# Seven block products for eight in 39 tiles of a feed-forward product, and TensorE makes the last shift

## The chip, the cores and the metric

One core of a Trainium2 chip runs the whole program. The metric is device microseconds for one execution, as the median of several runs. The program is a two-layer encoder in float32. TensorE (PE) gets each float32 operand as two parts: a high part `h` (the value cast to the matmul format) and a low part `lo` (what the cast lost). A product is the sum of three matmuls: high by high, low by high, high by low.

## The reference, cut to what matters

```python
DEPTH, D_MODEL, D_FF, SEQ, N_META = 2, 2048, 8192, 256, 16
def _layer(h, w_in, ..., ln1_w, ln1_b, w_ff1, w_ff2, ln2_w, ln2_b):
    ...                                             # projections, two mixers, output projection
    h = _layer_norm(DEEPNORM_ALPHA * h + mix, ln1_w, ln1_b)
    ff = jnp.einsum('blf,fd->bld', jnp.square(jax.nn.relu(jnp.einsum('bld,df->blf', h, w_ff1))), w_ff2)
    return _layer_norm(DEEPNORM_ALPHA * h + ff, ln2_w, ln2_b)
```

The case is about the last `einsum` of layer two, by `w_ff2`: 256 tokens by 8192 by 2048 columns. In layer two the 16 meta tokens are no longer carried, so there are 256 rows.

## The kernel before

**Stages.** Layer two's feed-forward runs in two halves of 4096 hidden columns. A half makes its hidden activations (`ev_f` squares the rectified result and splits it into the pairs `u[k]`, 32 chunks of 128 columns; in the listings they are called `y0` to `y15` and `u16` to `u31`), and then calls `across(u, half, g)` four times, once for each group `g` of 512 output columns. "The second product" below means these eight calls.

**A tile.** `across` runs over 16 weight tiles. A tile holds two chunks of 128 rows by 512 columns, 1024 floats in each of 128 partitions. For a tile, TensorE makes 12 matmuls of 512 columns: two token halves of 128, two chunks, three parts. Here the activations are the stationary operand (they are loaded as weights) and the weight tile streams. The results collect in two PSUM banks (`bank`, shown as `mm`), one for each token half. In half 0 each bank first gets the transposed residual from `acc` (L1056).

**How a tile comes in.** `weights()` keeps `lead` = 3 tiles made ahead. `made` asks for a DMA into `raw` (a ring of 3 buffers, used in turn, L189 and L193). Then ScalarE (ACT) casts `raw` into `wh` (L220), and VectorE (DVE) subtracts to make `wl` (L221); each of these has a ring of 4 buffers. So tile j can be cast when TensorE is done with the high part of tile j-4, and its DMA can be issued when DVE has made `wl` of tile j-3. The DMAs are issued by SyncE's queue (SP) in order, and every engine runs its instructions in order.

**What sets the order.** The code is recorded in program order and a scheduler lays it out for each engine. `pump(1, 0)` runs one step of the foreground work in `fg`: after a group of columns, `gather` moves the two banks into `acc` (ACT copies in half 0; in half 1 DVE adds, and takes the statistics `bn` and the multiplication by the gain row `grow`). `ln_rows` loads four gain rows and four bias rows over `x` tiles that are no longer needed.

**The end.** In the last call (half 1, g = 3) token half 1's matmuls of the last `HELD` = 3 tiles are held back. `finish(0, ...)` works on token half 0 while they run, and `finish(1, ...)` follows. A `finish` adds the bank, takes mean and variance, gets 1/sigma (`rs`) by two small ACT and three small DVE steps (`newton`), and then makes the four outputs: `gain * (-mean/sigma) + bias`, then `acc * rs +` that. That is eight DVE operations of 512 columns for token half 0; for token half 1, ACT and GpSimd (POOL) take a share.

Of the kernel before, what the change touches and what calls it, by code (L numbers as in the profile page):

```python
# [39 lines left out]
HELD = 3  # L40
# [5 lines left out]
TURNS = {True: "hwhwhwhwhwhwhwhw", False: "hlhlwwhlhlwwhlhlwwhlhlww"}  # L46

# [12 lines left out]
class Trunk:  # L60
# [93 lines left out]
    def order(self):  # L154

        i, first = self.i, [(), (WB // 2, WB)]
        for l in range(DEPTH):
# [7 lines left out]
            for half in range(2):  # L165
                groups += [(i["wff1"][l, 8 * half + g], [kind(True, "once") if half or g > 1 else ("all2", "own2")[last]] * 4)
                           for g in range(8)]
                groups += [(i["wff2"][l, half, g], [kind(True, "flat")] * 4) for g in range(4)]
# [5 lines left out]
            for w, kinds in groups:  # L174
                n = w.shape[0]
                for t in range(n):
                    yield w[t], (WB,), kinds[4 * t // n]
# [7 lines left out]
    def made(self, ap, ends, kind):  # L185
# [3 lines left out]
        raw = self.wp.tile([P, WB], F32, name="raw", tag="raw")  # L189
        wh, wl = (self.wp.tile([P, WIDE], F32R, name=nm, tag=nm, bufs=4) for nm in ("wh", "wl"))  # L190
        wh, wl = self.blocks(wh, *HIGHS[kind]), self.blocks(wl, *LOWS[kind])
# [5 lines left out]
        return wh, wl  # L197

# [683 lines left out]
    def tail(self, ps):  # L882
# [3 lines left out]
        with tc.tile_pool(name="u", bufs=1, reuse_waits="tile") as up:  # L886
            for k in range(4):
                self.ln_part(k, 0, ps[k])
# [6 lines left out]
            for half in range(2):  # L895
                u = [self.pair(self.yp, "y", k) if k < DC else self.pair(up, "u", k) for k in range(2 * DC)]

                def ev_f(k, ps, **how):
# [10 lines left out]
                    self.split(t, h[:, :n], lo[:, :n])  # L909
# [117 lines left out]
    def ln_rows(self):  # L1027

        ns = self.i["norm"]
        self.gains, self.biases = [], []  # L1030
        for g in range(4):
            for i, to in enumerate((self.gains, self.biases)):
                t = self.reuse(("grow", "brow")[i], 4 * i + g, F32)
                self.nc.sync.dma_start(t, bass.AP(ns.tensor, ns.offset + i * D + g * 512, [[0, P], [1, 512]]))
                to.append(t)
            yield
# [6 lines left out]

    def across(self, u, half, g):
# [3 lines left out]
        nc, mm, end = self.nc, self.nc.tensor.matmul, half and g == 3  # L1048
# [3 lines left out]
        tokens = [slice(h * P, h * P + P) for h in range(2)]  # L1052
        if not half:
            for h in range(2):
                for c in range(4):
                    mm(bank[h][:, c * P:c * P + P], lhsT=self.acc[:, 4 * g + c, tokens[h]], rhs=self.ident,  # L1056
                       is_transpose=True, start=not c, stop=False, skip_group_check=True)

        def products(k, both, part, h):
            for j in range(2):  # L1060
                hi, lo = (a[:, tokens[h]] for a in u[k + j])
                for v in (hi,) if part else (hi, lo):
                    mm(bank[h], lhsT=v, rhs=self.row(both[part], j), start=bool(half and k + j + part == 0 and v is hi),  # L1063
                       stop=k == 2 * DC - 2 and part + j == 2, skip_group_check=True)

        held = []
        for k in range(0, 2 * DC, 2):
            both = self.weights()
            for part in range(2):
                for h in range(2):  # L1070
                    if end and h and k >= 2 * DC - 2 * HELD:
                        held.append((k, both, part, h))
                    else:
                        products(k, both, part, h)
            if k % 4 == 2 and not held:
                self.pump(1, 0)
        if end:
            self.drain()
            self.finish(0, d, bank)
            for h in held:  # L1080
                products(*h)
            self.finish(1, d, bank)
# [3 lines left out]
    def gather(self, half, g, d, bank):  # L1086

        tt = self.nc.vector.tensor_tensor
        if half and not g:
            self.stats = [self.lp.tile([P, 4, 6], F32, name=f"bn{h}", tag=f"bn{h}") for h in range(2)]  # L1090
        for h in range(2):
            if half:
                tt(d[h], d[h], bank[h], ALU.add)
            else:
                self.nc.scalar.copy(d[h], bank[h])
            yield
        for h in range(2 * half):
            self.nc.vector.bn_stats(self.stats[h][:, g], d[h])
            yield
# [3 lines left out]
    def finish(self, h, d, bank):  # L1103
# [5 lines left out]
        t = lambda nm, c: self.lp.tile([P, c], F32, name=f"{nm}{h}", tag=f"{nm}{h}")  # L1109
        mv, rs, tn, nm = t("mv", 2), t("rs2", 1), t("tn2", 1), t("nm", 1)  # L1110
        v.tensor_tensor(d[h], d[h], bank[h], ALU.add)
        v.bn_stats(self.stats[h][:, 3], d[h])
        v.bn_aggr(mv, self.stats[h].rearrange("p g c -> p (g c)"))
        self.newton(rs, mv[:, 1:2], self.eps, tn)
        v.tensor_tensor(d[h], d[h], self.gains[3], ALU.mult)
        v.scalar_tensor_tensor(nm, mv[:, 0:1], -1.0, rs, ALU.mult, ALU.mult)
        for g in range(4):
            o, gain, bias = self.reuse("out", 8 + 4 * h + g, F32), self.gains[g], self.biases[g]
# [195 lines left out]
```

## Time and profile before

| | |
|---|---|
| median of 3 runs | 2323.63 us (2323.55 to 2324.35) |
| the profiled execution's own time | 2321.78 us |
| its span, first to last instruction | 2319.9 us |
| PE busy | 2295.1 us, 99% of the span |
| DVE busy, ACT busy | 1504.5 us (65%), 1216.8 us (52%) |
| mean granted TensorE clock | 0.997 |

The profile gives busy time by engine, groups of instructions by source line, who waited for whom, and a list in order of time. A row such as "1781.47 1.05 ACT L220 CAST wh<-raw" reads: start in us, duration in us, engine, line, operation, output from input. "x8" is eight merged instructions, whose time runs from the first's start to the last's end. The bracket at a row's end is the idle time before it and who ended it. A row's "[1.67 <-PE mm L1063]" thus says that the engine sat idle 1.67 us until the matmul of line 1063. Matmuls overlap, so a lone one shows its whole latency, and the rate is read from the distance between starts.

### The profile page before, as it was taken

To read this page: it belongs to the slowest core of one execution; us is meant where nothing else is said; L and a number is where in the kernel's file an instruction comes from. 1 tells how busy PE (TensorE), PEld (TensorE's weight loads), DVE (VectorE), ACT (ScalarE), POOL (GpSimd) and SP (SyncE) were. 2 spreads that over 40 slices of the span, in tenths; PEclk is the share of its full clock that TensorE was granted. 3 is DMA by queue.
4 is the path that set the end of the run, shared out by engine and by line. 5 is a ranking of instruction groups with operands and counts; after the bars stand their busy time and mean duration, and the time that the engine had idled before them with its cause. 6 is when DMAs were issued, how large, how long until landed. Compare 5 with 4: busy or idle time off the path is not lost.

```text
span 2319.9 us, 43983 instructions
## 1 busy us (share of the span) xinstructions
PE 2295.1 (99%) x17856; PEld 2161.9 (93%) x17856; DVE 1504.5 (65%) x2314; ACT 1216.8 (52%) x2082; POOL 159.5 (7%) x245
## 2 busy tenths in 40 slices
PE   9999999999999999999999999999999999999996
PEld 9999999999999999999999899989988888888885
DVE  5588878875544455547576887788765444665555
ACT  5666665564433344444456766656754344554332
POOL 0023210100000000000020122201000000000000
PEclk9999999999999999999999999999999999999998
DMA  8456665555555555555555557666666655657663
GB/s 268 156 165 183 203 194 178 178 176 181 181 178 179 180 181 179 179 181 181 178 178 165 174 173 219 207 187 188 187 193 197 191 191 183 198 190 227 201 194 124
DMA packets 129803, 431.84 MB, mean 186 GB/s; under 512 B 14776, under 2 KB 23224, under 8 KB 129600
## 3 DMA queue, kind: packets, MB, share of 16 engines
q1 hardware_dynamic: 126720, 421.69, 58.3%
q10 hardware_dynamic: 2880, 7.34, 0.8%
q8 instruction: 140, 2.29, 0.4%
q14 instruction: 63, 0.52, 0.1%
HBM read 420.58 MB, written 8.39 MB: 185 GB/s over the span
## 4 chain that ended last, share of the span: by engine, by line
PE 79%; DVE 3%; ACT 1%; issue 1%; DMA 0%; POOL 0%; ACTq 0%; DVEq 0%; POOLq 0%; SPq 0%
PE mm L255 43%; PE mm L267 15%; PE mm L1063 15%; PE bg L307 1%; PE mm L307 1%; PE bg L317 1%; PE mm L317 1%; DVE wl L221 1%; ACT wh L220 0%; DMA raw<-in_win 0%; DVE acc L1173 0%; DVE S L620 0%; PE bg L856 0%; ACT ns L761 0%; DVE out L1126 0%
## 5 line engine op out<-in xcount | busy, mean ns | idle before, releaser
L221 DVE TENSOR_TENSOR wl<-raw,wh 128x1024 fp32r<-128x1024 f32 (+1 forms) x770 | 939.2, 1224 | 647.7 <-ACT wh L220 598.6
L220 ACT CAST wh<-raw 128x1024 fp32r<-128x1024 f32 (+1 forms) x770 | 804.7, 1047 | 769.0 <-PE mm L255 375.3
L255 PE MATMUL mm<-x,wh 128*128 128x272 f32 (+3 forms) x4544 | 805.9, 294 | 0.0
L255 PEld LDWEIGHTS mm<-x,wh 128*128 128x128 f32 x4544 | 647.5, 188 | 15.2 <-DVE gtn L582 0.3
L255 PE MATMUL mm<-x,wl 128*128 128x272 f32 (+3 forms) x2432 | 520.2, 284 | 0.0
L255 PEld LDWEIGHTS mm<-x,wl 128*128 128x128 f32 x2432 | 391.0, 188 | 0.0
L255 PE MATMUL mm<-y,wh 128*128 128x272 f32 x1408 | 230.0, 285 | 0.0
L255 PEld LDWEIGHTS mm<-y,wh 128*128 128x128 f32 x1408 | 195.4, 188 | 0.0
L267 PE MATMUL mm<-x,wh 128*128 128x512 f32 x832 | 193.8, 390 | 0.0
L267 PEld LDWEIGHTS mm<-x,wh 128*128 128x128 f32 x832 | 154.3, 188 | 31.0
L255 PE MATMUL mm<-u,wh 128*128 128x272 f32 x1024 | 167.0, 285 | 0.0
L255 PE MATMUL mm<-y,wl 128*128 128x272 f32 x704 | 143.3, 285 | 0.0
L255 PEld LDWEIGHTS mm<-u,wh 128*128 128x128 f32 x1024 | 141.9, 188 | 0.0
L1063 PE MATMUL mm<-wh,u 128*128 128x512 f32 x512 | 126.9, 389 | 0.0
L1063 PE MATMUL mm<-wh,y 128*128 128x512 f32 x512 | 126.9, 390 | 0.0
L1063 PEld LDWEIGHTS mm<-wh,u 128*128 128x128 f32 x512 | 96.1, 188 | 19.9
L1063 PEld LDWEIGHTS mm<-wh,y 128*128 128x128 f32 x512 | 95.8, 188 | 19.7
L255 PEld LDWEIGHTS mm<-y,wl 128*128 128x128 f32 x704 | 110.1, 188 | 0.0
L255 PE MATMUL mm<-u,wl 128*128 128x272 f32 x512 | 104.2, 285 | 0.0
L267 PEld LDWEIGHTS mm<-x,wl 128*128 128x128 f32 x832 | 98.4, 188 | 2.0
L267 PE MATMUL mm<-x,wl 128*128 128x256 f32 x832 | 98.8, 276 | 0.0
L255 PEld LDWEIGHTS mm<-u,wl 128*128 128x128 f32 x512 | 80.1, 188 | 0.0
(291 smaller groups left out, 2327.7 us busy)
## 6 DMA issues: line engine op xcount, KB each, us to landing
raw<-in_wff SPq DMA_DIRECT2D x512, 512.0 KB, 3.7
raw<-in_win SPq DMA_DIRECT2D x190, 512.0 KB, 4.2
raw<-in_wout SPq DMA_DIRECT2D x64, 512.0 KB, 4.2
hop<-nt ACTq DMA_DIRECT2D x16, 384.0 KB, 2.3
np<-hop SPq DMA_DIRECT2D x64, 96.0 KB, 4.8
nb<-in_nab SPq DMA_DIRECT2D x16, 352.0 KB, 5.6
xraw<-in_xT SPq DMA_DIRECT2D x7, 272.0 KB, 5.6
grow<-in_norm SPq DMA_DIRECT2D x4, 256.0 KB, 6.1
```

The source lines that it names most:

```text
L220: self.nc.scalar.copy(h, r)
L221: self.wl = self.nc.vector.tensor_tensor(lo, r, h.bitcast(F32), ALU.subtract).ins
L255: mm(o, lhsT=self.block(w, j), rhs=rhs, start=first and not i, stop=last and i == len(TURNS[once]) - 1)
L267: self.nc.tensor.matmul(o, lhsT=self.block(both[j // 8][low], j % 8), rhs=rhs, start=first and not i + j, stop=bool(last and i and j == 15 ...
L307: self.nc.tensor.matmul(ps[g + m][:, :n], lhsT=self.block(parts[p][0], 4 * j + m if first else 2 * m + j), rhs=acts[k + j][parts[p][1]][:, ...
L317: self.nc.tensor.matmul(o, lhsT=self.block(both[low], i), rhs=rhs, start=not low and k + i % 2 == 0, stop=k == DC - 2 and i % 2 == 1 and n ...
L1063: mm(bank[h], lhsT=v, rhs=self.row(both[part], j), start=bool(half and k + j + part == 0 and v is hi), stop=k == 2 * DC - 2 and part + j = ...
```

## The change

In 39 of the 128 tiles of the second product (6 of 16 tiles in each call of half 0; 5 of 16 in the first three calls of half 1) the two token halves by two chunks by two column halves are multiplied by a scheme of seven block products instead of eight (Winograd's form of Strassen's). These tiles need sums of blocks. For the weights: the tile is read once as kind `quad` (three of its four 256-column blocks are cast and subtracted), then DVE makes four sums **in place in the same `raw` buffer**, and kind `sums` casts and subtracts all four. A special tile thus takes two places in the rings of `wh` and `wl`, but one in that of `raw`. For the activations: `combine` makes four differences of 128x128 blocks and splits them, one time for each special tile and half, while the first product runs. Two more PSUM banks (`bg`) take products that both column halves or token halves share, and `gather` puts them together on DVE. A special tile's matmuls are 21 of 256 columns; the 12 that need sums alternate with the 12 of 512 columns of the plain tile that follows.

At the end, the held tiles are 4 instead of 3, and `finish` is rewritten: the shift `gain * (-mean/sigma) + bias` is made by TensorE (one small matmul turns `nm`, then two matmuls for each output, from rows that `ln_rows` prepares on ACT and DVE). DVE is left with one operation of 512 columns for each output.

```diff
-HELD = 3
+HELD = 4
+FEWER = (6, 5)
+FIRST = 6
+def plan(half, g):
+    n = 0 if half and g == 3 else FEWER[half]
+    special = list(range(FIRST, FIRST + n))
...
+    out = [(plain.pop(0), False)]
+    for i, k in enumerate(special):
+        out.append((k, True))
+        more = (i + 1) * (DC - n - 1) // n - i * (DC - n - 1) // n
+        out += [(plain.pop(0), False) for _ in range(more)]
...
+                    for t, special in kinds:
+                        yield w[t], (WB,), "quad" if special else "flat"
+                        if special:
+                            yield w[t], (), "sums"
...
-        raw = self.wp.tile([P, WB], F32, name="raw", tag="raw")
+        if kind == "sums":
+            raw = self.quad
+        else:
+            raw = self.wp.tile([P, WB], F32, name="raw", tag="raw")
...
+    def four(self, kind, ap, raw, wh, wl):
+        nc, add = self.nc, lambda o, a, b: self.nc.vector.tensor_tensor(o, a, b, ALU.add)
+        q = [raw[:, i * Q:i * Q + Q] for i in range(4)]
+        if kind == "quad":
+            self.quad = raw
+            self.asked = nc.sync.dma_start(raw, ap).ins
+            at, names = slice(Q, WB), ("11", "22", "21")
+        else:
+            add(q[1], q[1], q[0])
+            add(q[0], q[0], q[2])
+            add(q[2], q[2], q[1])
+            add(q[3], q[3], q[2])
+            at, names = slice(0, WB), ("t3", "t1", "t2", "t4")
...
+        nc.scalar.copy(h, raw[:, at])
+        self.wl = nc.vector.tensor_tensor(lo, raw[:, at], h.bitcast(F32), ALU.subtract).ins
...
+                for p in special([(2, left, x[0], "11"), (0, left, x[1], "21"), (0, right, s["s4"], "22")], w):
+                    mm(*p)
+                w = self.weights()
+                first = special([(1, left, x[2], "t4"), (2, right, s["s1"], "t1"),
+                                 (3, left, s["s2"], "t2"), (3, right, s["s7"], "t3")], w)
+                other = self.weights()
...
+                for p in zip(first, second):
+                    mm(*p[0]), mm(*p[1])
...
     def gather(self, half, g, d, bank):
...
+        nc.scalar.copy(r[0], bank[2])
+        tt(n, r[0][:, left], bank[3][:, left], ALU.subtract)
+        tt(r[1][:, left], n, bank[3][:, right], ALU.subtract)
+        yield
+        tt(r[1][:, right], r[0][:, right], r[1][:, left], ALU.subtract)
+        tt(r[0][:, right], r[0][:, right], n, ALU.subtract)
+        yield
         for h in range(2):
             if half:
-                tt(d[h], d[h], bank[h], ALU.add)
-            else:
-                self.nc.scalar.copy(d[h], bank[h])
+                tt(d[h], d[h], r[h], ALU.add)
+            tt(d[h], d[h] if half else r[h], bank[h], ALU.add)
...
-            src = self.acc[:, 4 * g:4 * g + 4, :].rearrange("p c t -> p (c t)")[:, h * 512:h * 512 + 512]
...
-                v.scalar_tensor_tensor(o, gain, nm, bias, ALU.mult, ALU.add)
-                v.scalar_tensor_tensor(o, src, rs, o, ALU.mult, ALU.add)
...
+            for g in four:
+                nc.tensor.matmul(banks[g], lhsT=one[:64], rhs=self.biases[g][:64], start=True, stop=False)
+                nc.tensor.matmul(banks[g], lhsT=row, rhs=self.rows[g][:96], start=False, stop=True)
...
+                v.scalar_tensor_tensor(o, o, rs, banks[g], ALU.mult, ALU.add)
...
+        rs, nm = stats(0)
+        products(held[:18])
+        banks = shifts(0, nm)
+        products(held[18:])
+        rs1, nm1 = stats(1)
+        outputs(0, rs, banks)
+        outputs(1, rs1, shifts(1, nm1))
```

Three places of the recorded order show what stands where. The first is TensorE at the first tiles of half 0, g = 0. Names are tiles with their numbers: `wh_22026` and `wh_22032` are the first and second weight tile before; now `wh_22122` is the first, `wh_22128` the three plain blocks of the first special tile, `wh_22184` its four sums, and `wh_22205` the plain tile that follows; `cb` are the activations' differences. Before:

```order
L1063 MATMUL mm_22076<-wl_22027,y0_20120 128x512
L1063 MATMUL mm_22076<-wl_22027,y1_20121 128x512
L1063 MATMUL mm_22077<-wl_22027,y0_20120 128x512
L1063 MATMUL mm_22077<-wl_22027,y1_20121 128x512
L1063 MATMUL mm_22076<-wh_22032,y2_20122 128x512 x2
L1063 MATMUL mm_22076<-wh_22032,y3_20123 128x512 x2
L1063 MATMUL mm_22077<-wh_22032,y2_20122 128x512 x2
L1063 MATMUL mm_22077<-wh_22032,y3_20123 128x512 x2
```

And now, from the end of the same first tile:

```order
L1169 MATMUL mm_22173<-wl_22123,y1_20121 128x512
L1169 MATMUL bg_22174<-wh_22128,y12_20132 128x256 x2
L1169 MATMUL mm_22172<-wh_22128,y13_20133 128x256 x2
L1169 MATMUL mm_22172<-wh_22128,cb2_21160 128x256 x2
L1169 MATMUL bg_22174<-wl_22129,y12_20132 128x256
L1169 MATMUL mm_22172<-wl_22129,y13_20133 128x256
L1169 MATMUL mm_22172<-wl_22129,cb2_21160 128x256
L1169 MATMUL mm_22173<-wh_22184,y13_20133 128x256
L1169 MATMUL mm_22172<-wh_22205,y2_20122 128x512
L1169 MATMUL mm_22173<-wh_22184,y13_20133 128x256
L1169 MATMUL mm_22172<-wh_22205,y2_20122 128x512
```

Nine matmuls of 256 columns stand between two plain tiles, and from there the sums' matmuls alternate with those of the next plain tile, so that both tiles are needed at once.

The second place is DVE in half 1, while the results of g = 0 are gathered during g = 1. Before, one piece of `gather` stands after every second `wl`:

```order
L1093 TENSOR_TENSOR acc_18928<-acc_18928,mm_24972 128x512
L221 TENSOR_TENSOR wl_25321<-raw_25319,wh_25320 128x1024
L221 TENSOR_TENSOR wl_25339<-raw_25337,wh_25338 128x1024
L1093 TENSOR_TENSOR acc_18928<-acc_18928,mm_24973 128x512
L221 TENSOR_TENSOR wl_25358<-raw_25356,wh_25357 128x1024
L221 TENSOR_TENSOR wl_25376<-raw_25374,wh_25375 128x1024
L1098 BN_STATS bn0_25316<-acc_18928 128x6
```

Now (L248 is `four`, L233 its sums, L273 a plain tile's `wl`; `raw_26071` is one special tile's buffer and `raw_26146` the next one's, which is the same memory, since three `raw` are used in turn and two plain tiles stand between):

```order
L248 TENSOR_TENSOR wl_26073<-raw_26071,wh_26072 128x768
L1235 TENSOR_TENSOR rc1_26045<-rc0_26044,rc1_26045 128x256
L233 TENSOR_TENSOR raw_26071<-raw_26071 128x256
L1236 TENSOR_TENSOR rc0_26044<-rc0_26044,rn_26046 128x256
L233 TENSOR_TENSOR raw_26071<-raw_26071 128x256 x3
L248 TENSOR_TENSOR wl_26104<-raw_26071,wh_26103 128x1024
L1240 TENSOR_TENSOR acc_18928<-acc_18928,rc0_26044 128x512
L273 TENSOR_TENSOR wl_26127<-raw_26125,wh_26126 128x1024
L1241 TENSOR_TENSOR acc_18928<-acc_18928,mm_25601 128x512
L273 TENSOR_TENSOR wl_26142<-raw_26140,wh_26141 128x1024
L248 TENSOR_TENSOR wl_26148<-raw_26146,wh_26147 128x768
```

A special tile now puts six operations on DVE in a fixed order, with ACT's cast of the sums (`wh_26103`) between the last sum and the `wl` that reads it.

The third place is the end on DVE, after the last `wl`; before, eight operations of 512 columns stand between `nm0` and the second token half's first add (the `L1111` at the end):

```order
L1116 SCALAR_TENSOR_TENSOR nm0_26141<-mv0_26138,rs20_26139 128x1
L1125 SCALAR_TENSOR_TENSOR out8_26152<-grow0_25010,nm0_26141,brow4_25012 128x512
L1125 SCALAR_TENSOR_TENSOR out9_26156<-grow1_25050,nm0_26141,brow5_25052 128x512
L1126 SCALAR_TENSOR_TENSOR out8_26152<-acc_18928,rs20_26139,out8_26152 128x512
L1126 SCALAR_TENSOR_TENSOR out9_26156<-acc_18928,rs20_26139,out9_26156 128x512
L1125 SCALAR_TENSOR_TENSOR out10_26160<-grow2_25090,nm0_26141,brow6_25092 128x512
L1125 SCALAR_TENSOR_TENSOR out11_26164<-grow3_25130,nm0_26141,brow7_25132 128x512
L1126 SCALAR_TENSOR_TENSOR out10_26160<-acc_18928,rs20_26139,out10_26160 128x512
L1126 SCALAR_TENSOR_TENSOR out11_26164<-acc_18928,rs20_26139,out11_26164 128x512
L1111 TENSOR_TENSOR acc_18928<-acc_18928,mm_25873 128x512
```

Now (`bg_27113` to `bg_27116` are the banks with the shifts that TensorE made):

```order
L1263 SCALAR_TENSOR_TENSOR nm0_27079<-mv0_27076,rs20_27077 128x96
L1272 TENSOR_TENSOR nmr0_27110<-mm_27108,nmr0_27110 32x128
L1282 SCALAR_TENSOR_TENSOR acc_18928<-acc_18928,rs20_27077,bg_27113 128x512
L1282 SCALAR_TENSOR_TENSOR acc_18928<-acc_18928,rs20_27077,bg_27114 128x512
L1282 SCALAR_TENSOR_TENSOR acc_18928<-acc_18928,rs20_27077,bg_27115 128x512
L1259 TENSOR_TENSOR acc_18928<-acc_18928,mm_26807 128x512
L1282 SCALAR_TENSOR_TENSOR acc_18928<-acc_18928,rs20_27077,bg_27116 128x512
```

Between the two adds stand one small step and three operations of 512 columns; the fourth output of token half 0 comes after the second token half's add.

More of the change, by code (lines that the diff above doesn't have):

```diff
@@ L167, in order @@
                            for g in range(8)]
[L168 removed]
+                groups += [(i["wff2"][l, half, g], plan(half, g) if last else ["all"] * 4) for g in range(4)]
             if l == 0:
@@ L1059, in products @@
-        def products(k, both, part, h):
-            for j in range(2):
[L1061 to L1072, printed above, removed]
-                    else:
-                        products(k, both, part, h)
-            if k % 4 == 2 and not held:
+                    nc.tensor.matmul(bank[h][:, c * P:c * P + P], lhsT=self.acc[:, 4 * g + c, tokens[h]], rhs=self.ident,
+                                     is_transpose=True, start=not c, stop=False, skip_group_check=True)
```

176 lines of the change are left out of this document (139 added, 37 removed).

## The prediction, made before the changed kernel ran

> **What bounds the kernel now.** I read the page's busy times and chain first, then the second product in order of time, then who waits for whom there.
>
> ```profile
> PE 2295.1 (99%) x17856; PEld 2161.9 (93%) x17856; DVE 1504.5 (65%) x2314; ACT 1216.8 (52%) x2082; POOL 159.5 (7%) x245
> PE 79%; DVE 3%; ACT 1%; issue 1%; DMA 0%; POOL 0%; ACTq 0%; DVEq 0%; POOLq 0%; SPq 0%
> ```
>
> TensorE never stops: it is the bound, and every matmul saved would count, as long as what feeds TensorE keeps up. The windows show the stages that matter: half 0's first product, half 0's second, half 1's second, and the end.
>
> ```profile
> core 0: us, PE busy (x) PEld busy (x) DVE busy (x) ACT busy (x) POOL busy (x), PEclk, DMA share, GB/s
> 1660.00:1776.00 116.00, 116.00 (x680) 102.39 (x679) 75.94 (x112) 61.55 (x93) 0.00 (x0) 1.00 0.62 195
> 1776.60:1954.30 177.70, 177.70 (x799) 147.42 (x797) 79.88 (x68) 71.75 (x74) 0.00 (x0) 1.00 0.61 191
> 2128.10:2302.35 174.25, 174.25 (x769) 144.01 (x767) 91.18 (x93) 65.32 (x65) 0.00 (x0) 1.00 0.62 190
> 2302.35:2319.90 17.55, 0.00 (x0) 0.00 (x0) 13.33 (x21) 1.83 (x4) 3.29 (x2) 0.60 0.32 120
> ```
>
> In the second product DVE and ACT are half idle, which invites the change. But busy shares say nothing of how long one tile takes to pass through. In order of time:
>
> ```profile
> 1781.47 1.05 ACT L220 CAST wh<-raw 128x1024 fp32r<-128x1024 f32 x1 [1.67 <-PE mm L1063]
> 1782.13 1.98 PE L1063 MATMUL mm<-wh,y 128*128 128x512 f32 x8
> 1782.55 1.23 DVE L221 TENSOR_TENSOR wl<-raw,wh 128x1024 fp32r<-128x1024 f32 x1 [1.49 <-ACT wh L220]
> 1784.19 1.05 ACT L220 CAST wh<-raw 128x1024 fp32r<-128x1024 f32 x1 [1.67 <-PE mm L1063]
> 1785.27 1.23 DVE L221 TENSOR_TENSOR wl<-raw,wh 128x1024 fp32r<-128x1024 f32 x1 [1.49 <-ACT wh L220]
> ```
>
> A tile comes every 2.72 us (1784.19 less 1781.47), so a 512-column matmul takes 2.72/12 = 0.227. ACT always waits for TensorE to give back a `wh`, never for a transfer: there is slack. The transfer itself:
>
> ```profile
> SPq L193 <- DVE wl L221: 141.4, 60, 3.2
> ```
>
> ```profile
> DMA to landing us min/median/max: 3.2/3.5/4.5
> ```
>
> Each DMA waits for the `wl` that empties its buffer, and lands 3.2 to 4.5 us after its issue. With three `raw` and a tile each 2.72 us that is hidden.
>
> **Seven products for eight.** The 256-column rate, from layer two's output projection (where both the load and the matmul of 256 columns appear), and the page's single duration:
>
> ```profile
> 1537.30 1.07 PE L267 MATMUL mm<-y,wl 128*128 128x256 f32 x8
> ```
>
> ```profile
> L267 PE MATMUL mm<-x,wl 128*128 128x256 f32 x832 | 98.8, 276 | 0.0
> ```
>
> Eight take 1.07, the last shows 0.276 of latency: (1.07 - 0.276)/7 = 0.1134. A special tile is 21 x 0.1134 = 2.38 us of TensorE instead of 2.72; 39 tiles save 13.3 us. That is the most this part can give, and it comes only if TensorE need not wait.
>
> **The way of a special tile.** Now DVE and ACT do for it: cast of 768, `wl` of 768, four sums of 256 one after the other, cast of 1024, `wl` of 1024. The durations by size:
>
> ```profile
> L221 DVE TENSOR_TENSOR wl<-raw,wh 128x1024 fp32r<-128x1024 f32 x43 | 52.0, 1224 | 32.8 <-ACT wh L220 18.4 <-issue 13.4 <-PE mm L267 0.7
> L220 ACT CAST wh<-raw 128x1024 fp32r<-128x1024 f32 x42 | 44.2, 1052 | 24.3 <-DMA raw<-in_wff 10.3 <-PE mm L267 9.9 <-PE mm L317 3.4
> L343 DVE TENSOR_TENSOR u<-ft,u 128x256 fp32r<-128x256 f32 x15 | 6.3, 423 | 3.8 <-ACT u L342 3.8
> L342 ACT CAST u<-ft 128x256 fp32r<-128x256 f32 x15 | 6.1, 407 | 16.0 <-DVE ft L908 15.7
> L906 DVE TENSOR_TENSOR ft<-ft 128x256 f32<-128x256 f32 x4 | 1.7, 424 | 1.5 <-ACT ft L905 1.5
> ```
>
> On straight lines between 256 and 1024: cast of 768 0.83, `wl` of 768 0.955; a sum is 0.42. An operation that needs the one before it on DVE starts 0.04 after that one's end (first two rows of the end, below: 2298.30 + 0.69 to 2299.03), one that doesn't starts before that end:
>
> ```profile
> 2269.92 1.22 DVE L221 TENSOR_TENSOR wl<-raw,wh 128x1024 fp32r<-128x1024 f32 x1 [1.49 <-ACT wh L220]
> 2271.06 0.69 DVE L1098 BATCH_NORM_STATS2 bn<-acc 128x6 f32<-128x512 f32 x1
> ```
>
> so a `wl` passes the next on after 1.14. From ACT to DVE it is 0.03 (1784.19 + 1.05 to 1785.27).
>
> Since the sums are made in place, the buffer is held until the sums' `wl` is done. With two plain tiles between special ones, all of half 1 and every second gap of half 0, the next special tile uses the same buffer. From one sums' `wl` to the next: that `wl` 1.23, issue 0.03, transfer to cast 3.4, cast 0.83, 0.03, `wl` 0.955, four sums 0.04 + 4 x 0.42 + 3 x 0.04 = 1.84, to ACT 0.05, cast 1.05, 0.03: **9.45 us**. TensorE needs 2.38 + 2 x 2.72 = 7.82 for the same tiles. The wait sits on ACT's cast of 768; behind it in ACT's queue stand the casts of the sums and of both plain tiles, on SP the plain tiles' DMAs stand behind this one's, and TensorE waits for the sums' `wh`. For the transfer I take 3.4, between the stage's least and median: the three transfers of a round are now asked for within 2.3 us, then none for seven, so the special tile's finds the queue empty.
>
> [...]
>
> With one plain tile between, the next buffer is free, but DVE goes in order: `wl` 1.14, plain `wl` 1.14, `wl` of 768 and sums 0.955 + 1.84, cast between 1.13: **6.2 us**, against TensorE's 2.38 + 2.72 = 5.10. From a call's last special tile to the next call's first, the buffer is that of a plain tile: 1.14 + 9.45 = 10.6 (TensorE: 11.44 in half 0 with 0.9 of transposes, 10.54 in half 1).
>
> `gather` now has four DVE operations of 256 columns and two of 512 a call in half 0, eight of 512 in half 1: 3.1 and 7.2 us at 0.42 and 0.69. By the recorded order half of it lands after a sums' `wl`, under the wait for a transfer, and half between a `wl` of 768 and its sums or in the 6.2 gaps. I count 2.1 and 3.1 on the path; the ends are 0 and all. Its two further banks are read at the next call's start, and with two of four `bg` banks used in each call TensorE need not wait for them.
>
> - Half 0, each later call: 3 x 6.2 + 2 x 9.45 + 10.6 + 2.1 = 50.2, before 16 x 2.72 + 0.9 = 44.4: +5.8, three times, +17.4. The first call starts with tiles made ahead; adding the gaps from its start (second sums cast at 6.8, then 9.45, 6.2, 9.45, 6.2, the plain cast, 6.8 of products) gives 46.0: +1.6.
> - Half 1, calls 1 and 2: 4 x 9.45 + 10.6 + 3.1 = 51.5, before 43.5: +8.0 each, +16.
> - Half 1, call 0 has the loads of the gain and bias rows in its way.
>
> ```profile
> grow<-in_norm SPq DMA_DIRECT2D x4, 256.0 KB, 6.1
> ```
>
> ```profile
> 2130.16 1.05 ACT L220 CAST wh<-raw 128x1024 fp32r<-128x1024 f32 x1
> 2135.98 1.05 ACT L220 CAST wh<-raw 128x1024 fp32r<-128x1024 f32 x1 [4.76 <-DMA raw<-in_wff]
> ```
>
> Already now the tile queued behind four of them on SP is cast only 8.9 us after the product's start (2137.03 less 2128.10), hidden by the tiles ahead. Now the second special tile stands behind five loads and, on ACT, behind conversions of those rows that wait for the same loads. Cast end 9.9, then `wl` 1.0, two conversions 1.3 on DVE (32 x 512; bound by the 0.69 of 512 columns), sums 1.84, cast 1.1: 15.1 instead of the 11.6 at which TensorE could use it; three gaps of 9.45 + 1.3 and 6.8 of products: 54.2, **+10.8**. If no load holds anything, the cast is done at 9.2 and the call costs +4.7.
> - Half 1, call 3 has no special tile: 0.
>
> `combine` adds at most 8 operations of under 0.42 to DVE for two chunks, 3.4 us per 10.9. DVE is idle 35% in that stage (75.94 of 116.00), 3.8 us per 10.9; TensorE is three tiles ahead there. Cost 0; were the cover gone, each of the 11 pairs would cost a part of 3.4. The split of `raw` by name, `plan` and the host's reordering cost nothing.
>
> **The end.**
>
> ```profile
> 2298.30 0.69 DVE L1111 TENSOR_TENSOR acc<-acc,mm 128x512 f32<-128x512 f32 x1 [5.39 <-PE mm L1063]
> 2299.03 0.69 DVE L1112 BATCH_NORM_STATS2 bn<-acc 128x6 f32<-128x512 f32 x1
> 2301.26 0.16 DVE L1116 SCALAR_TENSOR_TENSOR nm<-mv,rs 128x1 f32<-128x1 f32 x1
> 2306.76 0.68 DVE L1111 TENSOR_TENSOR acc<-acc,mm 128x512 f32<-128x512 f32 x1
> 2314.34 1.63 DVE L1126 SCALAR_TENSOR_TENSOR out<-acc,rs,out 128x512 f32<-128x512 f32 x1
> ```
>
> From token half 0's add to the last output it is 17.7 us. Now: 18 held matmuls (4.08) cover the 3.1 of statistics; turning `nm` and four row matmuls bring the first output to 5.95; three outputs at 0.67 to 8.0; the second add and statistics with the fourth output inside, 3.8, to 11.8; turn, copy, subtract, matmul 1.55; four outputs 2.8: 16.2, so -1.5. One held tile more starts this 6 x 0.227 = 1.4 earlier. **-2.8**; bounds 0 and -4, since nothing here shows the small matmul or its copy.
>
> **Sum:** 1.6 + 17.4 + 10.8 + 16 - 2.8 = +43. On the profiled execution's 2321.78 that is 2364.8; the median shown is 1.85 above that execution, so 2366.6.
>
> **Rivals.** *The transfer hides after all (faster).* Place: the special tile's buffer. If its transfer took under 3.4 - (9.45 - 7.82) = 1.8 us, or the buffer came back early, only DVE's 6.2 gaps would stay, 1.1 each and half given back in the next gap. Then 13.3 and 2.8 are gained, less up to 8: 2308 to 2316. Against it: no transfer of the stage landed under 3.2, and the buffer's last reader is the sums' `wl`. 0.04.
> *Longer transfers.* Three asked for at once may share bandwidth: at the row's 4.5, 25 transfers on the path (11 and 14) add 1.1 each: 2394. 0.11, most of it inside the range.
> *TensorE slows down.* The window after the last matmul shows the clock at 0.60 with TensorE idle. If pauses of 1.6 to 3 us did the same, TensorE would be the bound again below 7.82/9.45 = 0.83 of full clock; at half, 7 calls of 42 would take 84 instead of 50: 2600. 0.03. [...]
>
> **Chances and range.** Forecast 0.79. Low end: transfers 3.2 (-5), `gather` all hidden (-12.5), no load in the way (-6): 2343, say 2342. High: 2394. A smaller loss than the low end, through slack that I don't see, has 0.03. A measurement of this kernel tells 0.2%, 4.6 us, from no change: faster 0.04, same 0.02, slower 0.94.
>
> **What would show it.** In the second product: TensorE idle for some 50 us in all; ACT's cast of 768 released by the DMA; sums' `wl` 9.4 apart in half 1, 6.2 and 9.4 by turns in half 0; granted clock 1.0; call 3 of half 1 unchanged; the end about 1.5 shorter from the first add. Casts of 768 released by TensorE instead, and no idle time, would prove the loop wrong.

## The result, and the profile after

The changed kernel takes 2378.83 us (median of 6; 2376.63 to 2379.52) against 2323.59 before (2321.76 to 2324.35): 1.0238 times as long, interval 1.0224 to 1.0251. It is slower by 55 us, where 43 were forecast (2366.6, range 2342 to 2394). The profiled execution took 2376.63 us. The page's busy times and chain of the kernel after:

```profile
PE 2311.3 (97%) x18227; PEld 2181.4 (92%) x18227; DVE 1636.4 (69%) x2643; ACT 1255.0 (53%) x2172; POOL 157.1 (7%) x243
PE 66%; DVE 9%; DMA 4%; ACT 4%; issue 2%; POOL 0%; ACTq 0%; DVEq 0%; POOLq 0%; SPq 0%
```

TensorE had 79% of the chain that ended last and has 66%; VectorE, ScalarE and the transfers took the rest. The windows of the kernel after (columns as before: busy times by engine, granted clock, DMA share, GB/s) are half 0's second product, half 1's first, and half 1's second:

```profile
1775.40:1981.00 205.60, 181.95 (x1027) 156.49 (x1026) 144.73 (x202) 85.83 (x94) 0.00 (x0) 1.00 0.51 162
1981.00:2153.40 172.40, 172.40 (x1016) 152.48 (x1015) 124.94 (x208) 92.90 (x146) 0.00 (x0) 1.00 0.65 199
2153.40:2356.00 202.60, 178.34 (x889) 150.19 (x888) 136.42 (x182) 80.39 (x89) 0.00 (x0) 0.97 0.52 162
```

TensorE now stands still about 24 us in each half of the second product, and the first product between them takes what it took. One round of the loop in half 1, call 0, in order of time (L248 is a special tile's `wl`, L233 its sums, L247 its casts, L1098 the conversions of the gain and bias rows):

```profile
2189.03 1.23 DVE L248 TENSOR_TENSOR wl<-raw,wh 128x1024 fp32r<-128x1024 f32 x1 [1.19 <-ACT wh L247]
2190.28 0.33 SPq L237 DMA_DIRECT2D raw<-in_wff  x1
2193.97 0.83 ACT L247 CAST wh<-raw 128x768 fp32r<-128x768 f32 x1 [3.08 <-DMA raw<-in_wff]
2194.84 0.96 DVE L248 TENSOR_TENSOR wl<-raw,wh 128x768 fp32r<-128x768 f32 x1 [2.32 <-ACT wh L247]
2195.83 0.68 DVE L1098 SCALAR_TENSOR_TENSOR wrow<-grow,wrow 32x512 fp32r<-32x512 f32 x1
2196.54 0.68 DVE L1098 SCALAR_TENSOR_TENSOR brow<-braw,brow 32x512 fp32r<-32x512 f32 x1
2197.26 1.80 DVE L233 TENSOR_TENSOR raw<-raw 128x256 f32<-128x256 f32 x4
2199.17 1.04 ACT L247 CAST wh<-raw 128x1024 fp32r<-128x1024 f32 x1 [4.36 <-DVE raw L233]
2200.25 1.23 DVE L248 TENSOR_TENSOR wl<-raw,wh 128x1024 fp32r<-128x1024 f32 x1 [1.19 <-ACT wh L247]
2200.27 0.79 PE L1169 MATMUL mm<-wh,u 128*128 128x256 f32 x2 [2.95 <-ACT wh L247]
```

The transfer is asked for 0.02 after the `wl` that empties the buffer (2189.03 + 1.23 to 2190.28), its cast starts 3.7 later, and the sums' `wl` comes 11.2 after the one before; TensorE stands 2.95. All special tiles, grouped by line and shape:

```profile
L247 ACT CAST wh<-raw 128x1024 fp32r<-128x1024 f32 x39 | 40.8, 1046 | 131.7 <-DVE raw L233 128.2 <-PE bg L1169 3.5
L248 DVE TENSOR_TENSOR wl<-raw,wh 128x768 fp32r<-128x768 f32 x39 | 37.3, 956 | 41.5 <-ACT wh L247 41.5
L247 ACT CAST wh<-raw 128x768 fp32r<-128x768 f32 x39 | 32.5, 834 | 67.6 <-DMA raw<-in_wff 62.3 <-PE bg L1169 3.0 <-DVE wl L273 1.3
```

The cast of 768 waits for its transfer (62.3 of 67.6 us), not for TensorE. The end on VectorE:

```profile
2354.83 0.69 DVE L1259 TENSOR_TENSOR acc<-acc,mm 128x512 f32<-128x512 f32 x1 [4.04 <-PE mm L1169]
2359.43 0.28 DVE L1272 TENSOR_TENSOR nmr<-mm,nmr 32x128 fp32r<-32x128 f32 x1 [1.39 <-ACT nmr L1271]
2360.68 2.07 DVE L1282 SCALAR_TENSOR_TENSOR acc<-acc,rs,bg 128x512 f32<-128x512 f32 x3 [0.97 <-PE bg L1276]
2368.41 2.72 DVE L1282 SCALAR_TENSOR_TENSOR acc<-acc,rs,bg 128x512 f32<-128x512 f32 x4 [0.89 <-PE bg L1276]
```

From the first add to the last output it is 16.30 us (2368.41 + 2.72 - 2354.83), against 17.67.

By stage, after less before: up to the second product -0.4; half 0 of it 202.8 against 177.1, **+25.7**; half 1's first product 0.0; half 1 up to the first add 201.4 against 170.2, **+31.2**, in which one more held tile saves 1.4; from there -1.4, and -0.4 behind the last VectorE operation. Together 54.7; the spans differ by 54.8.

### The profile page after: what moved, and what is told of

Same layout as the page of the kernel before. It is cut to its first block, busy times and chain, and to the rows that moved or that the text cites. A ratio compares the mean times of both kernels' runs of the same rounds, so it can differ in the third digit from the quotient of the medians.

```text
span 2374.7 us, 45220 instructions
## 1 busy us (share of the span) xinstructions
PE 2311.3 (97%) x18227; PEld 2181.4 (92%) x18227; DVE 1636.4 (69%) x2643; ACT 1255.0 (53%) x2172; POOL 157.1 (7%) x243
## 4 chain that ended last, share of the span: by engine, by line
PE 66%; DVE 9%; DMA 4%; ACT 4%; issue 2%; POOL 0%; ACTq 0%; DVEq 0%; POOLq 0%; SPq 0%
PE mm L307 42%; PE mm L319 15%; DMA raw<-in_wff 4%; PE mm L1169 3%; DVE raw L233 3%; ACT wh L247 2%; DVE wl L248 2%; DVE wl L273 1%; PE bg L359 1%; PE mm L359 1%; PE bg L369 1%; PE mm L369 1%; ACT wh L272 1%; DMA raw<-in_win 0%; DVE acc L1337 0%
## 5 line engine op out<-in xcount | busy, mean ns | idle before, releaser
L273 DVE TENSOR_TENSOR wl<-raw,wh 128x1024 fp32r<-128x1024 f32 (+1 forms) x731 | 889.5, 1223 | 475.1 <-ACT wh L272 447.1
L272 ACT CAST wh<-raw 128x1024 fp32r<-128x1024 f32 (+1 forms) x731 | 760.9, 1046 | 572.8 <-PE mm L307 352.5
L247 ACT CAST wh<-raw 128x768 fp32r<-128x768 f32 x78 | 73.3, 940 | 199.3 <-DVE raw L233 128.2
L248 DVE TENSOR_TENSOR wl<-raw,wh 128x768 fp32r<-128x768 f32 x78 | 85.1, 1091 | 87.7 <-ACT wh L247 87.7
L1169 PE MATMUL mm<-wh,u 128*128 128x512 f32 (+1 forms) x412 | 104.7, 380 | 33.7 <-ACT wh L247 33.7
L1169 PE MATMUL mm<-wh,y 128*128 128x512 f32 (+1 forms) x456 | 118.2, 386 | 14.2 <-ACT wh L247 12.5
L1169 PEld LDWEIGHTS mm<-wh,u 128*128 128x128 f32 x412 | 74.8, 193 | 50.6 <-ACT wh L247 38.6
L1169 PEld LDWEIGHTS mm<-wh,y 128*128 128x128 f32 x456 | 82.7, 190 | 32.0 <-ACT wh L247 14.8
```

The source lines that it names most:

```text
L247: nc.scalar.copy(h, raw[:, at])
L248: self.wl = nc.vector.tensor_tensor(lo, raw[:, at], h.bitcast(F32), ALU.subtract).ins
L272: self.nc.scalar.copy(h, r)
L273: self.wl = self.nc.vector.tensor_tensor(lo, r, h.bitcast(F32), ALU.subtract).ins
L1169: nc.tensor.matmul(bank[to][:, at], lhsT=v, rhs=w, start=to not in begun, stop=stop, skip_group_check=True)
```

## The experiments

Theory: a special tile holds its one `raw` buffer through transfer, two casts and the sums; where the next special tile gets the same buffer, the round through it (predicted 9.45 us) is longer than TensorE's work. Rivals: VectorE's and ScalarE's order is too slow whatever the buffers; the transfers are slow by themselves; the end or the row conversions cost something; TensorE's own work is dearer.

All ratios are to the kernel before, run on the same chip (its medians there: 2323.16, 2323.40 and 2322.08 us).

### The end alone

```diff
-FEWER = (6, 5)
+FEWER = (0, 0)
...                       # and the short gather of two banks
```

> All 128 tiles of the product are plain (no tile of seven products, two banks per call, the short gather); what stays of the change is the end: four tiles held back and the last shift made by TensorE, with the gain and bias rows it needs. By the buffer theory the whole loss sits in the special tiles, so this kernel stands where the end alone puts it: 1.4 us saved behind the first addition, 1.36 for the tile that was moved behind it, 0.4 at the very end, so 2320.5 us, 2318 to 2323. If instead the conversions of the gain and bias rows on ScalarE and VectorE cost something by themselves (the first call of half 1 lost most in the changed kernel), it is 2324 to 2332.

2319.63 us, 0.9987 (0.9978 to 0.9996). Both products' stages are as before (177.07 and 168.84, one held tile less), and the end is a gain of 3.5 us, with the conversions in it, inside the 2318 to 2323 that were expected. So the special tiles alone cost 2378.83 - 2319.63 = 59 us.

### A ring of their own for the special tiles

```diff
+        elif kind == "quad":
+            raw = self.up.tile([P, WB], F32, name="qraw", tag="qraw", bufs=2)
```

> The changed kernel, but the tiles of seven products are loaded into a ring of two buffers of their own, so the next one's transfer no longer waits for the sums of the one before; every instruction else is the same. Buffer theory: the distance between two sums' casts with two plain tiles between falls from 9.6 to 11 us to TensorE's 7.82; with one plain tile it stays at 6.2 to 6.3 in VectorE's order or falls towards 5.1 where the weights made ahead cover it; VectorE's own work in a two-tile gap is about 6.9 us and does not bind. The pauses of some 3 us go, and with them the falls of the granted clock. Time 2308 to 2324 us, most likely 2314. Rival, the chain of dependent casts and sums on ScalarE and VectorE is the bound whatever the buffers: two-plain gaps stay above 9 us and the time above 2350.

2325.71 us, 1.0009 (1.0 to 1.0018): 53 of the 59 us come back with no instruction taken away. It is 1.7 us above the range that was expected, and far from the rival's 2350. The group of the casts of 768 in this kernel:

```profile
L249 ACT CAST wh<-qraw 128x768 fp32r<-128x768 f32 x39 | 32.4, 832 | 9.9 <-PE bg L1171 4.0 <-ACT wh L274 3.1 <-PE mm L321 1.5
```

Their 67.6 us of waiting are 9.9, and no transfer is among the main causes. One of the pauses that are left, in order of time:

```profile
1888.40 1.23 DVE L250 TENSOR_TENSOR wl<-qraw,wh 128x1024 fp32r<-128x1024 f32 x1 [1.19 <-ACT wh L249]
1888.42 0.50 PE L1171 MATMUL mm<-wh,u 128*128 128x256 f32 x2 [0.52 <-ACT wh L249]
```

The likeliest value was 2314, though: TensorE still pauses, 0.15 to 0.56 us each time, behind ScalarE's casts of the sums and of plain tiles, and VectorE stands 1.19 behind the cast of the sums; and TensorE's own work is dearer than I had priced it, as the next kernel shows.

### TensorE's change without the weights' work

The special tiles' own loads, casts and sums are left out; their products read quarters of the next plain tile, so the output is another.

```diff
-                        yield w[t], (WB,), "quad" if special else "flat"
-                        if special:
-                            yield w[t], (), "sums"
+                        if not special:
+                            yield w[t], (WB,), "flat"
...
+                other = w
+                w = dict(zip(("11", "22", "21", "t3", "t1", "t2", "t4"), [[o[0](q * Q, [[P, 2]]) for o in other] for q in (0, 1, 2, 3, 0, 1, 2)]))
```

> Leaves the 39 special tiles' own loads, casts and sums out: their 21 products of 256 columns read quarters of the plain tile that follows, so TensorE's instructions are those of the changed kernel and the weights' way (transfer, ScalarE, VectorE) is relieved; the output is another. Any theory in which TensorE only waits in the changed kernel: TensorE's saving shows in full, 39 x 0.34 = 13.3 us and the end's 3.2, so 2307 us, 2305 to 2312. If the 21 short products take longer than their 0.1134 us each (two alternating lists of operands, changing banks), the time is above 2315 and TensorE itself is part of the loss.

2313.4 us, 0.996 (0.9948 to 0.9973), above the 2305 to 2312 that were expected. TensorE never waits here in the second product, so with the end's 3.5 taken off, 39 special tiles are worth 6.2 us, not 13.3. Rows of TensorE in this kernel, in order of time:

```profile
1786.55 0.40 PE L1168 MATMUL bg<-wh,y 128*128 128x256 f32 x2
1788.43 0.40 PE L1168 MATMUL mm<-wh,y 128*128 128x512 f32 x1
1788.67 0.28 PE L1168 MATMUL bg<-wh,cb 128*128 128x256 f32 x1
1788.79 0.40 PE L1168 MATMUL mm<-wh,y 128*128 128x512 f32 x1
1791.84 1.32 PE L1168 MATMUL mm<-wh,y 128*128 128x512 f32 x5
```

From a special tile's first product to the next plain tile's first it is 5.29 us (1791.84 - 1786.55), where 2.38 + 2.72 = 5.10 was predicted. Over all records a product of 256 columns takes 0.118 to the next (0.1134 was priced), and one of 512 takes 0.233 where a short one follows, 0.227 otherwise; why the short ones are slower here than in the projection no run shows. 21 x 0.118 + 12 x 0.0063 = 2.55: a special tile saves 0.17.

### Three special tiles a call

```diff
-FEWER = (6, 5)
+FEWER = (3, 3)
```

> Three tiles of seven products per call instead of six and five (21 in all, with four plain tiles between two of them), the ring of three buffers as in the changed kernel. Buffer theory: the loop of about 9.7 us lies beside TensorE's 2.38 + 4 x 2.72 = 13.3 us and is hidden, so each special tile gives its 0.34 us: 21 x 0.34 = 7.1, with the end's 3.2 less what the four-bank gather costs in 7 calls (0 to 1 each): 2313 us, 2310 to 2321. Rival, each special tile costs a fixed amount (54.7 us over 39 tiles, 1.5 us each, the end's gain set apart): 21 x 1.5 = 31 more, 2350.

2328.07 us, 1.0021 (1.0013 to 1.003): a miss by 15 us, and the flat price was further off. Half 0 has no pause, as the theory says, and takes 175.5 us (before 177.1): 1.6 less, near 12 x 0.17 and not the 12 x 0.34 of the forecast. Half 1 takes 179.1 against 168.8 with the end alone. The second call of half 1 at its start, in order of time:

```profile
2184.68 0.84 ACT L247 CAST wh<-raw 128x768 fp32r<-128x768 f32 x1 [0.17 <-DMA raw<-in_wff]
2187.86 0.68 DVE L1241 TENSOR_TENSOR acc<-acc,mm 128x512 f32<-128x512 f32 x1
2188.45 0.68 DVE L1240 TENSOR_TENSOR acc<-acc,rc 128x512 f32<-128x512 f32 x1
2189.39 0.68 DVE L1241 TENSOR_TENSOR acc<-acc,mm 128x512 f32<-128x512 f32 x1
2191.43 1.04 ACT L247 CAST wh<-raw 128x1024 fp32r<-128x1024 f32 x1 [5.91 <-DVE raw L233]
2192.53 0.39 PE L1169 MATMUL mm<-wh,y 128*128 128x256 f32 x1 [1.61 <-ACT wh L247]
```

The transfer is there in time, but on VectorE a plain tile's `wl` and pieces of the four-bank `gather` stand before and among the sums, and the cast of the sums comes 6.8 after the cast of 768 (2191.43 - 2184.68; 0.84 + 0.96 + 1.80 and some 0.2 between them would be 3.8). In call 0 the row conversions stand there. TensorE's pauses in half 1 add up to 8.2 us, where I had priced 0 to 1 a call; how they divide between the two causes this run does not show.

### No sums

The four sums are left out; the second cast reads the raw quarters, so the output is another.

```diff
-            add(q[1], q[1], q[0])
-            add(q[0], q[0], q[2])
-            add(q[2], q[2], q[1])
-            add(q[3], q[3], q[2])
```

> The changed kernel without the four sums in place on VectorE (1.8 us per special tile): the second cast and subtraction read the raw quarters; transfers, casts, products and the ring of three are as they were; the output is another. Loop through the buffer: about 9.7 - 1.84 = 7.9 us with two plain tiles between, against TensorE's 7.8 to 8.0; with one plain tile 4.4 against 5.2; between calls 10.1 against 10.5. So nearly all of the loss goes: 2325 us, 2319 to 2335. Rival, the transfers themselves are slow because they queue behind each other on SyncE's queue and the sums count for nothing: most of the loss stays, above 2355.

2314.08 us, 0.9963 (0.9949 to 0.9976): with the same ring and the same transfers, the whole loss goes, and TensorE is busy 173.40 of 173.40 us in half 0. 1.84 us less in a round bring it from 9.7 to 7.9, under TensorE's 8.0. Slow transfers by themselves are out. It is 5 us below the range that was expected: I had counted on more pauses from the conversions.

### One own buffer

```diff
+        elif kind == "quad":
+            raw = self.up.tile([P, WB], F32, name="qraw", tag="qraw", bufs=1)
```

> The changed kernel with one buffer of its own for the special tiles beside the plain tiles' three, so one buffer more than the changed kernel has in all. Loop theory: with two plain tiles between, a ring of three gives the next special tile just the buffer of the one before, so those distances stay at 9.6 to 10.4 us; with one plain tile between, where the ring of three gave another buffer and the distance was 6.3 to 6.9, the single buffer now puts the whole loop there too: 12 distances of the first half grow by some 3.2 us each, 38 in all, and the boundary between calls (11.9) falls by up to 1.4 in seven places. Time 2407 to 2417 us, slower with one more buffer. Rival, there are too few buffers altogether for the transfers: one more helps, below 2365.

2407.61 us, 1.0364 (1.0349 to 1.0378): one buffer more, and 29 us slower than the changed kernel, as only the loop theory has it. In half 0 of this kernel, in order of time, with one plain tile between:

```profile
1815.39 1.23 DVE L250 TENSOR_TENSOR wl<-qraw,wh 128x1024 fp32r<-128x1024 f32 x1 [1.19 <-ACT wh L249]
1816.53 1.22 DVE L275 TENSOR_TENSOR wl<-raw,wh 128x1024 fp32r<-128x1024 f32 x1
1816.64 0.33 SPq L239 DMA_DIRECT2D qraw<-in_wff  x1
1820.27 0.83 ACT L249 CAST wh<-qraw 128x768 fp32r<-128x768 f32 x1 [3.96 <-DMA qraw<-in_wff]
1822.13 1.81 DVE L235 TENSOR_TENSOR qraw<-qraw 128x256 f32<-128x256 f32 x4
1825.12 1.23 DVE L250 TENSOR_TENSOR wl<-qraw,wh 128x1024 fp32r<-128x1024 f32 x1 [1.19 <-ACT wh L249]
1825.14 0.74 PE L1171 MATMUL mm<-wh,u 128*128 128x256 f32 x2 [2.38 <-ACT wh L249]
```

It is 9.73 from one sums' `wl` to the next (1825.12 - 1815.39), with the one plain tile's `wl` (L275) between; in the changed kernel this distance was 6.26. All such distances within half 0's calls are now 9.6 to 10.3, whether one plain tile stands between or two.

### The row conversions in the last call

```diff
...                                                 # ln_rows keeps the loads alone
+    def ln_conv(self):                              # the 16 conversions
...
+            if half and g == 2:
+                self.fg.append(self.ln_conv())
```

> The changed kernel with the conversions of the gain and bias rows (8 activations of 0.63 us, 8 subtractions of 0.68 us) moved from the first call of the second half to the last call, which has no special tile; the rows are loaded where they were. If the conversions delay the loop of the first call (its distances were 13.73, 11.13, 11.09, 11.22 us, against 10.1 to 11.5 in the two calls behind it), 4 to 5 us come back: 2374 us, 2370 to 2376. If the eight row loads on SyncE's queue are the cause, nothing changes: 2377 to 2381.

2372.32 us, 1.0214 (1.02 to 1.0228): 6.5 us come back, all in half 1 (194.9 against 201.4), more than the 4 to 5 expected. Distances in call 0 were 13.7, 11.1, 11.1, 11.2 and are 12.8, 9.6, 9.6, 9.7: the last three lose what the two subtractions before the sums took (1.43 in the rows of the changed kernel, 2195.83 to 2197.26). The loads stayed where they were, so they are not the cause of what came back. The 12.8 is left: there the special tile's transfer, asked for behind five row loads, takes 6.7 us to its cast. No run takes the loads away.

### Another order on VectorE, with the old ring and with an own one

The sums stand right behind the first `wl`, then the next plain tile, and the cast and `wl` of the sums last.

```diff
                     for t, special in kinds:
                         yield w[t], (WB,), "quad" if special else "flat"
-                        if special:
+                        if due:
                             yield w[t], (), "sums"
+                        due = special
...
         self.wl = nc.vector.tensor_tensor(lo, raw[:, at], h.bitcast(F32), ALU.subtract).ins
+        if kind == "quad":
+            add(q[1], q[1], q[0])
...                                                 # all four sums stand here now
```

With the ring of three buffers:

> The new order on VectorE alone, with the ring of three buffers as in the changed kernel. Loop theory: VectorE's subtraction of the next plain tile (1.23 us) takes the place of the wait for ScalarE's cast (1.19), so a special tile holds its buffer as long as before: distances of 9.6 to 10.4 with two plain tiles between, and the time within 2370 to 2385. Rival, VectorE's order is the cause and the ring only helped it: most of the loss goes, below 2345.

2344.23 us, 1.009 (1.0074 to 1.0105): outside the theory's range, and by its number just inside the rival's (below 2345), with 35 of the 59 us back. But the buffers changed too; this kernel in order of time:

```profile
1831.40 1.22 DVE L276 TENSOR_TENSOR wl<-raw,wh 128x1024 fp32r<-128x1024 f32 x1
1832.65 0.33 SPq L239 DMA_DIRECT2D raw<-in_wff  x1
1833.21 0.42 DVE L235 TENSOR_TENSOR raw<-raw 128x256 f32<-128x256 f32 x1
1835.49 1.23 DVE L246 TENSOR_TENSOR wl<-raw,wh 128x1024 fp32r<-128x1024 f32 x1 [1.19 <-ACT wh L245]
```

The next special tile's DMA (1832.65) goes out right behind the plain tile's `wl`, while the sums are still running: in this order the plain tile gives its buffer back first, and the program hands that one on. In the buffers of the built program the special tiles, with two plain ones between, read "Q0 p1 p2 Q1", where the changed kernel has "Q0 p2 p1 Q0". So the edit changed two things at once; it does not test VectorE's order by itself, and bears out neither side. Half 0 takes 186.4 us and half 1 182.7 (202.8 and 201.4 in the changed kernel).

With an own ring of two:

> The special tiles' own ring of two buffers, and another order on VectorE: the four sums straight behind the first subtraction of the special tile, the following plain tile's cast and subtraction next, and the cast and subtraction of the sums last, so that VectorE does not stand 1.19 us behind ScalarE's cast of the sums. Theory: with the buffers out of the way VectorE's own order is next (0.95 + 1.80 + 1.19 + 1.23 + 2 x 1.23 = 7.6 us and the gather's pieces against TensorE's 7.9), and the short pauses of 0.3 to 0.9 us that were left with the ring alone go: TensorE's own time (2313.4 us in the run without the special tiles' weight work) and some 3 us for the row conversions in the second half's first call: 2316 us, 2313 to 2320. Rival, ScalarE's casts set the pauses whatever VectorE's order: 2323 or more.

2319.15 us, 0.9981 (0.9972 to 0.999). Half 0 takes 173.4, the time of TensorE's work alone: VectorE's wait for ScalarE was what the ring had left there. Half 1 keeps five pauses in call 0, beside the conversions.

### All three together, and the products one after the other

The ring of two, the new order and the conversions in the last call:

> Own ring of two buffers, the new order on VectorE, and the row conversions in the last call. If all three reasons hold, TensorE waits for nothing in the product and the time is that of the run in which only TensorE's work was changed: 2314 us, 2312 to 2318. If the gather of four banks costs by itself in seven calls, 2318 to 2324.

2313.62 us, 0.9962 (0.9949 to 0.9974). The windows of this kernel's second product, half 0 and half 1, show TensorE busy throughout:

```profile
1776.00:1949.40 173.40, 173.40 (x1012) 152.44 (x1011) 141.01 (x200) 87.26 (x93) 0.00 (x0) 1.00 0.62 195
2123.90:2290.70 166.80, 166.79 (x881) 143.27 (x880) 134.43 (x180) 81.46 (x89) 0.00 (x0) 1.00 0.62 190
```

Then the 12 short and 12 long products in turns were put one after the other:

```diff
-                for p in zip(first, second):
-                    mm(*p[0]), mm(*p[1])
+                for p in second + first:
+                    mm(*p)
```

> The fastest version so far (own ring, new order on VectorE, conversions in the last call), with the special tile's 12 products of 256 columns and the next plain tile's 12 of 512 one after the other instead of in turns. In the runs so far TensorE's distance from a 512-column product to the next is 226.7 us per thousand, but 233.3 where a 256-column one follows, and 117.5 to 118 from a 256-column one to the next. If the turns cost that 6.5 ns each, 12 x 6.5 ns x 39 = 3.0 us come off: 2310.6 us, 2309 to 2312. If the weight load behind a short product then shows (256 behind 256 above 118), nothing or a loss: 2313 to 2318.

2311.24 us, 0.9951 (0.9938 to 0.9963), the fastest: 10.8 us below the kernel before on its chip. The product's stages are 172.1 and 165.8 us, 2.3 less than in turns together (3.0 expected). The intervals of the two whole times overlap; it is the stages that show the difference.

## Why the prediction was right, and where its sizes were off

The side, the mechanism and the range held: the ring of their own, the single buffer and the kernel without sums each move the time as a round through the held buffer does, and in opposite directions. By its steps:

- **The round, 9.45.** Bare rounds are 9.6 to 9.9 (half 0, call 0: 9.89 and 9.68). Every duration in it was met (0.83, 0.96, 1.80, 1.04, 1.23); the term that was short is the transfer, issue to cast mostly 3.5 to 3.8 (three times 4.0 to 5.0) where 3.4 was taken. The next plain tile's transfer follows it by 1.1 to 1.7 us, so it has the queue to itself only at its start; that this is the cause was not tested.
- **One plain tile between, 6.2.** 6.26.
- **From call to call, 10.6.** 11.8 to 12.05 in half 0. There the special tile's transfer is asked for right behind a plain tile's, and takes 4.6 to 4.8 to the cast. This and the two rounds of a call (9.89 and 9.68) make 1.3 + 0.7 of the 1.9 us by which calls 1 to 3 (mean 52.1) exceed the 50.2 of the sum, and the small terms cancel; half 0 is +25.7 instead of +19.0.
- **`gather`, 2.1 and 3.1 on the path.** In half 0 the distances within calls 1 to 3 are together 1.6 to 2.1 above call 0's bare ones (6.26, 9.89, 9.68): right. Half 1's calls 1 and 2 take 56.0 and 53.3, where 51.5 was the sum. Within them the four distances are 4.3 and 2.6 above four bare ones of 9.65, mean 3.5: near the 3.1, and one of them (11.5) holds a transfer of 5.0. The rest is the distance from the call before, 13.1 and 12.0 where 10.6 was taken. In the one of 13.1 no piece of `gather` stands on VectorE; ScalarE's copy of a `bg` bank waits 4.52 us there for TensorE, whose granted clock was 0.50 from 2199.63 to 2206.46, and the casts stand behind that copy (rows below). In the kernel with the late conversions, whose granted clock is 1.00 from 2155 to 2205 us, this distance is 12.3.
- **Half 1, call 0: +10.8.** What is left of half 1's +32.6 (31.2 and the 1.4 of the held tile) without calls 1 and 2 (12.5 and 9.8) is 10.3. The reason was half right: the conversions count 6.5; what the loads count was not tested.
- **The end, -2.8.** -3.1 by stages, and -3.5 as a kernel of its own (0.9978 to 0.9996).
- **13.3 us at most from TensorE.** 6.2. This did not enter the sum, where the round sets the time, but with it the rival "the transfer hides" would have come out at 2313.4 instead of 2308. The failed step is the price of 0.1134 from a run of equal products; 0.118, and 0.006 more for a long product followed by a short one, were measured.
- **The clock.** "Granted clock 1.0" failed in half 1 (0.97 in the window: three falls to 0.50, 13.7 us together), nearly without the loss that the rival gave: but for the distance of 13.1, TensorE was not what set the round. The kernel before has short pauses too: after its start TensorE has seven of 0.3 to 0.6 us there, and one of 2.42 at 340.50 behind which the clock stays at 1.00.

ScalarE in the changed kernel between calls 0 and 1 of half 1, in order of time:

```profile
2206.64 0.59 ACT L1231 COPY rc<-bg 128x512 f32<-128x512 f32 x1 [4.52 <-PE bg L1169]
2207.12 1.05 ACT L272 CAST wh<-raw 128x1024 fp32r<-128x1024 f32 x1
2208.07 0.84 ACT L247 CAST wh<-raw 128x768 fp32r<-128x768 f32 x1
```

What is open: how much of half 1's excess in the changed kernel is `gather`, how much the row loads and how much contention among transfers; no run separated them there. Of the 12 us by which the forecast stood low, 6.7 lie in half 0 and 5.8 in half 1.

## What to carry to other kernels

A tile that is worked on in place keeps its buffer as long as the longest chain behind it; add up that chain, from the release to the next release, and compare it with what the bound engine does between two tiles of that buffer, not with busy shares. One more buffer can make it slower (one own buffer, +29 us) and a changed order can take away part of the loss by handing on another buffer (35 of 59 us), so look at which buffer comes next. Fewer multiplications in smaller pieces gain less than the count says: here 0.17 us of 2.72, not 0.34.

## What the runs showed of the hardware

Granted clock and pauses. With the single own buffer 11 pauses of TensorE in half 0 are 2.36 to 2.38 us long, and in nine stretches of 25 us or less from 1800 to 2015 us the granted clock is 0.77 to 0.97. Behind the pause before the row at 1825.14 above two products of 256 columns take 0.74, where 0.50 stands behind a pause with the ring of two; behind the one of 2.37 before 1805.64 the products of 256 columns come 0.21 us apart instead of 0.118. The window of that half, whose granted clock is the 0.89:

```profile
1777.50:2015.00 237.50, 202.55 (x1012) 171.23 (x1010) 143.25 (x200) 84.35 (x92) 0.00 (x0) 0.89 0.43 142
```

The distances there (9.6 to 10.3) are those of the changed kernel's bare rounds (9.6 to 9.9), whose half 0 has a granted clock of 1.00, so the lower clock cost next to nothing in this loop.

The length of a pause alone does not decide. In half 1 of the changed kernel the clock falls to 0.50 at pauses of 2.00, 2.95 and 2.36 us and not at others of 2.75, 2.35, 2.47 and 2.41; half 0 has 15 pauses from 0.81 to 1.97 at a granted clock of 1.00, but with the late conversions the same half's window has 0.99. What tells them apart was not shown: no run was made for it.
